# A hybrid encoder layer: norm weights, the left half of x tile 0 and three weight tiles per partition in one first transfer, issued by halves of the partitions on two queues

## The chip, the core and the metric

One Trainium2 chip, one of its cores. The metric is device time of one execution in microseconds (us), the median of several runs; the output must agree with the reference. The engines named below are TensorE (PE; its weight loads are shown apart, as PEld), VectorE (DVE), ScalarE (ACT), GpSimd (POOL) and SyncE (SP). Transfers are issued by SP, ACT or POOL and run on 16 DMA engines.

## The reference

One layer of a hybrid encoder on x of 512 positions by 1024 channels, in float32. The part that this change touches is the first norm and the start of the input projection:

```python
def rms_norm(x, g):
    xf = x.astype(jnp.float32)
    y = xf * lax.rsqrt(jnp.mean(xf * xf, axis=-1, keepdims=True) + EPS)
    return (y * g.astype(jnp.float32)).astype(x.dtype)
...
h = rms_norm(x, attn_norm_g[l])
proj = h @ w_in[l]          # 1024 x 2560
xr, gate, q, k, v = jnp.split(...)
```

Behind it come, in this order, a depthwise convolution and two gated linear recurrences (forward and backward) on xr, dilated attention with a relative bias on q, k and v, an output projection with residual, an MLP (1024 to 4096, squared ReLU, back to 1024) with residual, and a last norm.

## The kernel before

**Tiling.** Positions are on the free dimension (S = 512), channels on the partitions (P = 128), so x is eight channel tiles (KD = 8), each 128 x 512. The norm's gains are multiplied into x tile by tile; the division by the root mean square is done later, on the product.

**Three matmuls for one.** Each float32 operand is split into two parts of a narrower matmul format (FR): hi is the operand copied into that format, lo is the rest. A product is the sum hi x hi, hi x lo and lo x hi, three matmuls into the same accumulator in PSUM (`mm3`, lines 311 to 314). The order of every engine's work is written out by hand (a manual schedule for PE, ACT, DVE and POOL); each queue runs in program order.

**The start.** Lines 131 to 142 set constants, run one small Exp on ACT (`warm`, line 138, which brings a table load with it) and eight 128 x 128 warm-up matmuls of ones on PE (line 142; each shows as two passes). SP issues, in this order: line 335, x tile 0 and the eight gain columns (XG = 520 elements per partition) into the buffer `tw`; line 336, three 128-column weight tiles of channel tile 0 into the rest of the same buffer; line 339, the fourth weight tile (`w03`); line 341, x tile k with its three weight tiles, for k = 1 to 7. POOL copies the gains aside (`ag`, line 337).

**`cvx(k)`** (lines 347 to 368) makes the hi and lo parts of x tile k and of its weight tiles, on ACT and DVE. For k = 0: the hi part of x is made by halves, the left 256 columns on ACT (line 353) and the right 256 on DVE (line 354); the hi parts of weight tiles 0 and 1 on DVE (356), of tile 2 on ACT (357); then DVE subtracts for lo of x (363), lo of the three weight tiles (364) and, after ACT's copy of the fourth tile (366), its lo (367). `sq(k)` (372) squares x tile k on ACT for the mean square, `addsq` (375) adds the squares on DVE.

**The first projection** (lines 448 to 458) fills four PSUM accumulators `pxr[0..3]`, each 128 output channels by 512 positions. For k = 0 and 1 the order is: the three hi x hi matmuls of pxr[0..2], then the three hi x lo, then the three lo x hi (line 453); for k = 0 then the three of pxr[3] through `mm3`. For k of 2 and above, `mm3` for each of pxr[0..2].

The host lays the arrays out: `xw0` (line 1777) is the array that the transfers of lines 335 and 336 read.

Of the kernel before, what the change touches and what calls it, by code (L numbers as in the profile page):

```python
# [12 lines left out]
FT = mybir.dt.float32  # L13
FR = mybir.dt.float32r
AF = mybir.ActivationFunctionType
OP = mybir.AluOpType

P = 128
S = 512
D = 1024  # L20
KD = D // P
# [14 lines left out]
TH = S // 2  # L36
# [62 lines left out]
def hybrid_kernel(ctx: ExitStack, tc, xw0, xw, xn, w_in, w_v, w_out, w_up, w_dn, gates, vecs, bias, fg, out):  # L99
    nc = tc.nc  # L100
# [3 lines left out]
    work = ctx.enter_context(tc.tile_pool(name="work", bufs=1))  # L104
# [4 lines left out]
    act = nc.scalar.activation  # L109
    stt = nc.vector.scalar_tensor_tensor  # L110
    NG = 45

    def g_(name, dt=FT, shape=(P, S)):
        return work.tile(list(shape), dt, name=name, tag="g", bufs=NG)
# [4 lines left out]
    def ps_(name, tag):  # L119
        return psum.tile([P, S], FT, name=name, tag=tag, bufs={"pj": 4, "gs": 2, "et": 2}[tag])  # L120

    def f(t):
        return t.bitcast(FT)
# [7 lines left out]
    epsb = consts.tile([P, 1], FT, name="epsb")  # L131
# [3 lines left out]
    mhalf = consts.tile([P, 4], FT, name="mhalf")  # L135
    nc.gpsimd.memset(mhalf, -0.5)
    warm = consts.tile([P, 1], FT, name="warm")
    act(warm, epsb, AF.Exp)
    pwarm = ps_("pwarm", "et")
    one = nc.const_aps.tensor(1.0, [P, P], FT)  # L140
    for _ in range(8):
        nc.tensor.matmul(pwarm[:, :P], lhsT=one, rhs=one, start=True, stop=True)

    def softplus_consts():
# [166 lines left out]
    def mm3(o, a, b, first, last, on=False):  # L311
        nc.tensor.matmul(o, lhsT=a[0], rhs=b[0], start=bool(first), stop=False, skip_group_check=on)  # L312
        nc.tensor.matmul(o, lhsT=a[0], rhs=b[1], start=False, stop=False, skip_group_check=on)  # L313
        nc.tensor.matmul(o, lhsT=a[1], rhs=b[0], start=False, stop=bool(last), skip_group_check=on)  # L314
# [8 lines left out]
    h_hi = big.tile([P, KD, S], FR, name="h_hi", tag="bigA")  # L323
    h_lo = big.tile([P, KD, S], FR, name="h_lo", tag="bigB")

    XW, XG = S + 3 * P, S + KD
    ag = consts.tile([P, KD], FT, name="ag")
    xwt, w3 = [], []
    for k in range(KD):
        if 4 <= k < 7:  # L330
            xwt.append(stream.tile([P, 1024], FT, name="wraw", tag="wraw", bufs=3)[:, :XW])
        else:
            xwt.append(work.tile([P, 1024], FT, name="tw", tag="tw", bufs=4)[:, :XW if k else XG + 3 * P])
        if k == 0:
            nc.sync.dma_start(xwt[0][:, :XG], xw0[:, :XG])
            nc.sync.dma_start(xwt[0][:, XG:], xw0[:, XG:])
            nc.gpsimd.tensor_copy(ag, xwt[0][:, S:XG])
            w03 = g_("w03")[:, :P]
            nc.sync.dma_start(w03, w_in[3][:, :P])
        else:  # L340
            nc.sync.dma_start(xwt[k], xw[k - 1])
        if k == 6:
            nc.sync.dma_start(vt, vecs)

    sqx = {}

    def cvx(k):
        x, w = xwt[k][:, :S], xwt[k][:, S if k else XG:]
        g = ag[:, k:k + 1] if k else xwt[0][:, S:S + 1]
        hi, lo = g_("w3h", FR), g_("w3l", FR)  # L350
        if k < 2:
            c = (2 * P, 3 * P)[k]
            act(h_hi[:, k, :c], x[:, :c], AF.Copy, scale=g)
            nc.vector.tensor_scalar(h_hi[:, k, c:], x[:, c:], g, None, op0=OP.mult)
            if k == 0:
                nc.vector.tensor_copy(hi[:, :2 * P], w[:, :2 * P])
                act(hi[:, 2 * P:3 * P], w[:, 2 * P:], AF.Copy)
            else:
                nc.vector.tensor_copy(hi[:, :3 * P], w)
        else:  # L360
            act(h_hi[:, k, :], x, AF.Copy, scale=g)
            act(hi[:, :3 * P], w, AF.Copy)
        stt(h_lo[:, k, :], x, g, f(h_hi)[:, k, :], op0=OP.mult, op1=OP.subtract)
        nc.vector.tensor_tensor(lo[:, :3 * P], w, f(hi)[:, :3 * P], op=OP.subtract)
        if k == 0:
            act(hi[:, 3 * P:], w03, AF.Copy)
            nc.vector.tensor_tensor(lo[:, 3 * P:], w03, f(hi)[:, 3 * P:], op=OP.subtract)
        w3.append((hi, lo))

    def sq(k):  # L370
        sqx[k] = g_("sqx")
        act(sqx[k], xwt[k][:, :S], AF.Square)

    def addsq(k):
        nc.vector.tensor_tensor(sqx[0], sqx[0], sqx.pop(k), op=OP.add)

    cvx(0)
    sq(0)
    for k in range(1, KD):
        cvx(k)  # L380
        if 5 <= k < 7:
            next(spc)
        sq(k)
        if k >= 2:
            addsq(k - 1)
# [7 lines left out]
    def hk(k):  # L393
        return (h_hi[:, k, :], h_lo[:, k, :])

    def wk(c, k):
        if c < 3 or (c, k) == (3, 0):
            return tuple(t[:, c * P:(c + 1) * P] for t in w3[k])
        hi, lo = splits[c]
        return (hi[:, k * P:(k + 1) * P], lo[:, k * P:(k + 1) * P])  # L400
# [26 lines left out]
    def turned(ss, tag):  # L427
        pc = ps_("pcs", tag)
        for tt in range(4):
            nc.tensor.transpose(pc[:, tt * P:(tt + 1) * P], ss[:, tt * P:(tt + 1) * P], ident)  # L430
        return pc
# [16 lines left out]
    pxr = {t: ps_("pxr", "pj") for t in range(4)}  # L448
    for k in range(KD):
        if k < 2:  # L450
            for i, (a, b) in enumerate(((0, 0), (0, 1), (1, 0))):
                for t in range(3):
                    nc.tensor.matmul(pxr[t], lhsT=wk(t, k)[a], rhs=hk(k)[b], start=i == 0 and k == 0, stop=False)
            if k == 0:
                mm3(pxr[3], wk(3, 0), hk(0), True, False)
            continue
        for t in range(3):
            mm3(pxr[t], wk(t, k), hk(k), False, k == KD - 1)
            if k == KD - 1 and t == 0:
                sqt = turned(sqx[0], "et")  # L460

# [28 lines left out]
    xc, gt, gact = {}, {}, {}  # L490
# [252 lines left out]
    for n, (k, tt) in enumerate(steps):  # L743
        c = C_V + k // 2
        if k == 0:
            pv[tt] = ps_("pv", vtag[tt])
        hi, lo = splits[c]
# [511 lines left out]
    for w in OSEQ:  # L1259
        for i in range(4):  # L1260
            tt, k = i // 2, i % 2
# [260 lines left out]
    for half in range(2):  # L1522
# [5 lines left out]
        start = 0  # L1528
        if half == 0:
            start = 3  # L1530
# [161 lines left out]
        for j in range(7 * NQ):  # L1692
            _, w, q = seq[j]
# [32 lines left out]
        if half == 1:  # L1726
            b = 6 * NQ
# [89 lines left out]
```

## Time and profile before

| | us |
|---|---|
| median of 3 runs | 525.14 (524.99 to 525.32) |
| the profiled execution | 525.49 |
| its span, first to last instruction | 523.7 |
| PE busy | 517.1 (99%) |
| DVE busy | 430.4 (82%) |
| ACT busy | 352.2 (67%) |

The profile is of one execution. A row of its timeline reads: start, duration (both in us), engine, line of the kernel, operation, the tile written and those read, shapes, how many instructions were merged into the row, and in brackets the idle time just before with what ended it. SPq and ACTq are the instruction queues of SP and ACT, which show the issue of a transfer, not its data. Matmuls overlap, since they are pipelined, so that their starts tell the pace better than their durations. Before PE's first matmul and after its last one the span holds about 7.7 us in all.

### The profile page before, as it was taken

The numbers are of one execution on the slowest core, as the hardware profiler recorded it, in microseconds if no ns is written. First come the engines' busy times: TensorE is split into PE (matmuls) and PEld (weight loads), VectorE is DVE, ScalarE is ACT, GpSimd is POOL, SyncE is SP. The second block draws the span as 40 slices with busy tenths as digits, with TensorE's granted clock in tenths as the row PEclk, the third lists the DMA queues.
The fourth block names the chain that finished last, engine by engine and source line by source line (L and its number), as shares of the span: only waits on it lengthen the run. The fifth ranks groups of instructions, "written<-read, shape, count | busy, mean of one in ns | idle before, by whom it ended". The sixth has DMA issues, their size and how long they took to land.

```text
span 523.7 us, 8216 instructions
## 1 busy us (share of the span) xinstructions
PE 517.1 (99%) x3021; PEld 444.3 (85%) x3021; DVE 430.4 (82%) x668; ACT 352.2 (67%) x570; POOL 65.3 (12%) x89
## 2 busy tenths in 40 slices
PE   9999999999999999999999999999999999999995
PEld 8867888778777788899999888889999999888884
DVE  6899986788886898898789987789766978986885
ACT  7579946667857857586578666565667577655655
POOL 0173000000000321001300312001100300131000
PEclk9999999999999999999999999999999999999999
DMA  7636555266796499947595899976986497799704
GB/s 288 208 99 196 161 160 180 83 191 199 190 294 197 115 196 247 353 134 195 139 223 143 213 273 281 306 271 161 300 256 168 117 224 210 157 289 257 195 1 161
DMA packets 40329, 105.15 MB, mean 201 GB/s; under 512 B 5056, under 2 KB 13376, under 8 KB 40288
## 3 DMA queue, kind: packets, MB, share of 16 engines
q1 hardware_dynamic: 32448, 78.10, 44.5%
q0 software_dynamic: 7696, 26.32, 27.3%
q8 instruction: 24, 0.39, 0.3%
q10 hardware_dynamic: 144, 0.20, 0.1%
q14 instruction: 17, 0.14, 0.1%
HBM read 95.59 MB, written 4.29 MB: 191 GB/s over the span
## 4 chain that ended last, share of the span: by engine, by line
PE 99%; DVE 0%; issue 0%; DVEq 0%; ACT 0%; ACTq 0%
PE pu L314 10%; PE pu L312 10%; PE pu L313 10%; PE pd L314 10%; PE pd L312 10%; PE pd L313 10%; PE pqk L312 3%; PE pqk L314 3%; PE pqk L313 3%; PE pwo L312 3%; PE pwo L314 3%; PE pwo L313 3%; PE pav L942 2%; PE pt L842 2%; PE ps L806 2%; PE pp L312 1%
## 5 line engine op out<-in xcount | busy, mean ns | idle before, releaser
L269 DVE TENSOR_TENSOR wlo<-wraw,whi 128x1024 fp32r<-128x1024 f32 x71 | 86.6, 1220 | 24.0 <-ACT whi L247 23.9
L247 ACT ACTIVATE whi<-wraw 128x1024 fp32r<-128x1024 f32 x67 | 70.8, 1057 | 37.4 <-PE pd L314 18.4
L313 PE MATMUL pd<-wlo,ah 128*128 128x512 f32 (+1 forms) x195 | 75.2, 386 | 0.0
L312 PE MATMUL pd<-whi,ah 128*128 128x512 f32 (+1 forms) x195 | 75.2, 386 | 0.0
L314 PE MATMUL pd<-whi,al 128*128 128x512 f32 (+1 forms) x195 | 75.2, 386 | 0.0
L313 PE MATMUL pu<-hl,whi 128*128 128x256 f32 x224 | 63.4, 283 | 0.0
L314 PE MATMUL pu<-hh,wlo 128*128 128x256 f32 x224 | 63.4, 283 | 0.0
L312 PE MATMUL pu<-hh,whi 128*128 128x256 f32 x224 | 63.4, 283 | 0.0
L312 PE MATMUL pu<-h2h,whi 128*128 128x256 f32 (+1 forms) x200 | 60.1, 300 | 0.0
L313 PE MATMUL pu<-h2l,whi 128*128 128x256 f32 (+1 forms) x200 | 60.0, 300 | 0.0
L314 PE MATMUL pu<-h2h,wlo 128*128 128x256 f32 (+1 forms) x200 | 60.0, 300 | 0.0
L269 DVE TENSOR_TENSOR wlo<-tw,whi 128x1024 fp32r<-128x1024 f32 x37 | 45.2, 1221 | 17.7 <-ACT whi L247 17.7
L247 ACT ACTIVATE whi<-tw 128x1024 fp32r<-128x1024 f32 x38 | 40.1, 1058 | 24.9 <-PE pd L314 6.3
L312 PEld LDWEIGHTS pu<-hh,whi 128*128 128x128 f32 x224 | 43.0, 192 | 0.0
L313 PEld LDWEIGHTS pu<-hl,whi 128*128 128x128 f32 x224 | 43.0, 192 | 0.0
L314 PEld LDWEIGHTS pu<-hh,wlo 128*128 128x128 f32 x224 | 43.0, 192 | 0.0
L313 PEld LDWEIGHTS pd<-wlo,ah 128*128 128x128 f32 x195 | 36.6, 188 | 7.4
L312 PEld LDWEIGHTS pd<-whi,ah 128*128 128x128 f32 x195 | 36.6, 188 | 7.3
L314 PEld LDWEIGHTS pd<-whi,al 128*128 128x128 f32 x195 | 36.6, 188 | 7.4
L247 ACT ACTIVATE whi<-ts 128x1024 fp32r<-128x1024 f32 x24 | 25.4, 1060 | 25.2 <-PE pd L314 16.4
L313 PEld LDWEIGHTS pu<-h2l,whi 128*128 128x128 f32 x200 | 38.3, 191 | 1.3
L314 PEld LDWEIGHTS pu<-h2h,wlo 128*128 128x128 f32 x200 | 38.3, 191 | 1.3
(280 smaller groups left out, 1220.1 us busy)
## 6 DMA issues: line engine op xcount, KB each, us to landing
wraw<-in_w_up_dram SPq DMA_DIRECT2D x25, 512.0 KB, 4.8
ts<-in_w_dn_dram POOLq DMA_DIRECT2D x24, 512.0 KB, 13.5
wraw<-in_w_dn_dram SPq DMA_DIRECT2D x24, 512.0 KB, 8.7
tw<-in_w_up_dram SPq DMA_DIRECT2D x15, 512.0 KB, 6.7
tw<-in_w_up_dram POOLq DMA_DIRECT2D x15, 512.0 KB, 7.5
wraw<-in_w_in_dram SPq DMA_DIRECT2D x13, 512.0 KB, 4.3
ts<-in_w_dn_dram SPq DMA_DIRECT2D x8, 512.0 KB, 9.0
tw<-in_w_dn_dram SPq DMA_DIRECT2D x8, 512.0 KB, 7.0
```

Source lines behind the costliest of these rows:

```text
L247: act(hi, raws[i], AF.Copy)
L269: nc.vector.tensor_tensor(lo, r, f(splits[i][0]), op=OP.subtract)
L312: nc.tensor.matmul(o, lhsT=a[0], rhs=b[0], start=bool(first), stop=False, skip_group_check=on)
L313: nc.tensor.matmul(o, lhsT=a[0], rhs=b[1], start=False, stop=False, skip_group_check=on)
L314: nc.tensor.matmul(o, lhsT=a[1], rhs=b[0], start=False, stop=bool(last), skip_group_check=on)
L806: nc.tensor.matmul(psq[p, u][e][:, :NK], lhsT=qs_[p, a][r, P * qt:P * qt + P], rhs=kks[p][r, b, w:w + NK], start=i == 0, stop=i == 2)
L842: nc.tensor.transpose(pt[:, i * P:(i + 1) * P], en[h][qt][:, k:k + P], ident)
L942: nc.tensor.matmul(pav[p][a, co], lhsT=vs[:, jt, h * DH:(h + 1) * DH], rhs=et[h, jt][:, ci], start=jt == 0 and i == 0, stop=jt == 3 and i ...
```

## The change

- The host array `xw0` is laid out anew: the eight gain columns first, then the left half of x tile 0 (TH = 256 columns), the three weight tiles (384 columns), then the right half of x tile 0 and the fourth weight tile.
- The first transfer takes gains, left half and three weight tiles (XL = 648 elements, 2592 B per partition). Partitions 0 to 63 are issued by SP, partitions 64 to 127 by ACT. The small Exp that was first on ACT comes after ACT's issue.
- SP's second transfer brings the right half of x tile 0 and the fourth weight tile (384 elements per partition) into a buffer of its own, `x0r`. There is no third one: the x tiles 1 to 7 follow directly.
- For k = 0 the hi part of the left half of x is made on DVE and that of the right half on ACT; the hi part of weight tile 0 on ACT, of tiles 1 and 2 on DVE. The lo part of x and the squares are made in two halves.
- The three hi x hi matmuls of k = 0 become six of 256 columns: left halves of pxr[0..2], then right halves. The first of them alone clears the accumulator (`start`).
- Seven warm-up matmuls instead of eight.

```diff
-    act(warm, epsb, AF.Exp)
...
-    for _ in range(8):
+    for _ in range(7):
         nc.tensor.matmul(pwarm[:, :P], lhsT=one, rhs=one, start=True, stop=True)
...
-    XW, XG = S + 3 * P, S + KD
+    XW, XL = S + 3 * P, KD + TH + 3 * P
...
         if k == 0:
-            nc.sync.dma_start(xwt[0][:, :XG], xw0[:, :XG])
-            nc.sync.dma_start(xwt[0][:, XG:], xw0[:, XG:])
-            nc.gpsimd.tensor_copy(ag, xwt[0][:, S:XG])
-            w03 = g_("w03")[:, :P]
-            nc.sync.dma_start(w03, w_in[3][:, :P])
+            x0r = g_("x0r")
+            nc.sync.dma_start(xwt[0][:P // 2], xw0[:P // 2, :XL])
+            nc.scalar.dma_start(xwt[0][P // 2:], xw0[P // 2:, :XL])
+            act(warm, epsb, AF.Exp)
+            nc.sync.dma_start(x0r[:, :TH + P], xw0[:, XL:])
+            nc.gpsimd.tensor_copy(ag, xwt[0][:, :KD])
+            x0, w03 = (xwt[0][:, KD:KD + TH], x0r[:, :TH]), x0r[:, TH:TH + P]
...
+    lr = (slice(0, TH), slice(TH, S))
...
     def cvx(k):
...
+        if k == 0:
+            nc.vector.tensor_scalar(h_hi[:, k, lr[0]], x0[0], g, None, op0=OP.mult)
+            act(hi[:, :P], w[:, :P], AF.Copy)
+            nc.vector.tensor_copy(hi[:, P:3 * P], w[:, P:])
+            act(h_hi[:, k, lr[1]], x0[1], AF.Copy, scale=g)
+            for c, xc in zip(lr, x0):
+                stt(h_lo[:, k, c], xc, g, f(h_hi)[:, k, c], op0=OP.mult, op1=OP.subtract)
...
     def sq(k):
         sqx[k] = g_("sqx")
-        act(sqx[k], xwt[k][:, :S], AF.Square)
+        for c, xc in zip(lr, x0) if k == 0 else ((slice(0, S), xwt[k][:, :S]),):
+            act(sqx[k][:, c], xc, AF.Square)
...
             for i, (a, b) in enumerate(((0, 0), (0, 1), (1, 0))):
+                if i == k == 0:
+                    for c in lr:
+                        for t in range(3):
+                            nc.tensor.matmul(pxr[t][:, c], lhsT=wk(t, 0)[0], rhs=hk(0)[0][:, c], start=c is lr[0], stop=False, skip_group_check=True)
+                    continue
...
-    arrs["xw0"] = cont(np.concatenate([xT[0], cols(a["attn_norm_g"][0]), wx[0]], axis=1))
+    arrs["xw0"] = cont(np.concatenate([cols(a["attn_norm_g"][0]), xT[0][:, :TH], wx[0], xT[0][:, TH:], wi[:P, 3 * P:4 * P]], axis=1))
```

More of the change, by code (lines that the diff above doesn't have):

```diff
@@ L332, in hybrid_kernel @@
         else:
-            xwt.append(work.tile([P, 1024], FT, name="tw", tag="tw", bufs=4)[:, :XW if k else XG + 3 * P])
+            xwt.append(work.tile([P, 1024], FT, name="tw", tag="tw", bufs=4)[:, :XW if k else XL])
         if k == 0:
-            nc.sync.dma_start(xwt[0][:, :XG], xw0[:, :XG])
-            nc.sync.dma_start(xwt[0][:, XG:], xw0[:, XG:])
-            nc.gpsimd.tensor_copy(ag, xwt[0][:, S:XG])
-            w03 = g_("w03")[:, :P]
-            nc.sync.dma_start(w03, w_in[3][:, :P])
+            x0r = g_("x0r")
[5 more added lines that the diff above has]
+            x0, w03 = (xwt[0][:, KD:KD + TH], x0r[:, :TH]), x0r[:, TH:TH + P]
         else:
@@ L345, in hybrid_kernel @@
     sqx = {}
+    lr = (slice(0, TH), slice(TH, S))
     def cvx(k):
-        x, w = xwt[k][:, :S], xwt[k][:, S if k else XG:]
-        g = ag[:, k:k + 1] if k else xwt[0][:, S:S + 1]
+        x, w = (xwt[k][:, :S], xwt[k][:, S:]) if k else (None, xwt[0][:, KD + TH:])
+        g = ag[:, k:k + 1] if k else xwt[0][:, :1]
         hi, lo = g_("w3h", FR), g_("w3l", FR)
-        if k < 2:
-            c = (2 * P, 3 * P)[k]
+        if k == 0:
[5 more added lines that the diff above has]
+                stt(h_lo[:, k, c], xc, g, f(h_hi)[:, k, c], op0=OP.mult, op1=OP.subtract)
+        elif k == 1:
+            c = 3 * P
             act(h_hi[:, k, :c], x[:, :c], AF.Copy, scale=g)
             nc.vector.tensor_scalar(h_hi[:, k, c:], x[:, c:], g, None, op0=OP.mult)
[L355 to L359, printed above, removed]
+            nc.vector.tensor_copy(hi[:, :3 * P], w)
         else:
@@ L362, in cvx @@
             act(hi[:, :3 * P], w, AF.Copy)
-        stt(h_lo[:, k, :], x, g, f(h_hi)[:, k, :], op0=OP.mult, op1=OP.subtract)
+        if k:
+            stt(h_lo[:, k, :], x, g, f(h_hi)[:, k, :], op0=OP.mult, op1=OP.subtract)
         nc.vector.tensor_tensor(lo[:, :3 * P], w, f(hi)[:, :3 * P], op=OP.subtract)
@@ L451, in hybrid_kernel @@
             for i, (a, b) in enumerate(((0, 0), (0, 1), (1, 0))):
+                if i == k == 0:
[3 more added lines that the diff above has]
+                    continue
                 for t in range(3):
-                    nc.tensor.matmul(pxr[t], lhsT=wk(t, k)[a], rhs=hk(k)[b], start=i == 0 and k == 0, stop=False)
+                    nc.tensor.matmul(pxr[t], lhsT=wk(t, k)[a], rhs=hk(k)[b], start=False, stop=False, skip_group_check=True)
             if k == 0:
@@ L457, in hybrid_kernel @@
         for t in range(3):
-            mm3(pxr[t], wk(t, k), hk(k), False, k == KD - 1)
+            mm3(pxr[t], wk(t, k), hk(k), False, k == KD - 1, True)
             if k == KD - 1 and t == 0:
```

## The prediction

> **What bounds the kernel now.** I read the page first (span, busy shares, the chain that ended last), then the waits of PE, then the chain in order of time at its two ends.
>
> ```profile
> span 523.7 us, 8216 instructions
> PE 517.1 (99%) x3021; PEld 444.3 (85%) x3021; DVE 430.4 (82%) x668; ACT 352.2 (67%) x570; POOL 65.3 (12%) x89
> PE 99%; DVE 0%; issue 0%; DVEq 0%; ACT 0%; ACTq 0%
> PE pwarm L142 <- PEq L1806: 0.8, 1, 0.8
> 516.82 0.48 DVE x1n L1473
> 519.87 0.33 DVEq L1813
> ```
>
> The chain is PE from end to end. The only wait that PE shows is the 0.8 us before its first warm-up matmul; after the last matmul about 7 us of DVE, ACT and output are left. So the time is: when PE gets to its first useful matmul, plus a queue of matmuls without gaps, plus a tail. The change touches only the first of these, and a shift there should reach the end unreduced, since no later stage is seen to hold PE up. The rest is decided in the first 9 us, on PE (start, duration, engine, line, then what it writes and reads):
>
> ```profile
> 0.73 3.49 PEld L142 LDWEIGHTS pwarm<-const-float32-1.0 128*128 128x128 f32 x16 [0.73 <-issue]
> 4.41 0.93 PEld L453 LDWEIGHTS pxr<-h_hi,w3h 128*128 128x128 f32 x3 [0.18 <-ACT w3h L357]
> 4.44 1.62 PE L453 MATMUL pxr<-h_hi,w3h 128*128 128x512 f32 x3
> 5.00 1.05 PE L453 MATMUL pxr<-h_hi,w3h 128*128 128x512 f32 x2
> 5.85 1.34 PE L453 MATMUL pxr<-h_lo,w3h 128*128 128x512 f32 x3
> 6.28 0.91 PE L453 MATMUL pxr<-h_lo,w3h 128*128 128x512 f32 x2
> 7.03 0.84 PE L453 MATMUL pxr<-h_hi,w3l 128*128 128x512 f32 x3
> 8.39 0.84 PE L453 MATMUL pxr<-h_hi,w3h 128*128 128x512 f32 x3
> 9.07 0.84 PE L453 MATMUL pxr<-h_lo,w3h 128*128 128x512 f32 x3
> ...
> 6.00:7.00 1.00, 1.00 (x4) 0.79 (x3) 0.49 (x2) 0.62 (x2) 0.00 (x0) 1.00 1.01 380
> ```
>
> Durations overlap, so I go by starts. From 5.85 to 6.28 one matmul of 512 columns takes 0.43 us; from 8.39 to 9.07 three take 0.68, which is 0.227 each. So the array runs at about half speed until some 6.9 us (between 6.28 and 7.03 the pitch changes), although the window row for 6 to 7 us gives a granted clock of 1.00 (the value ahead of the DMA share 1.01): here the pitch is what counts. And from 4.41 on PE is dense: its weight loads wait 0.18 us for the ACT cast of line 357, never again. A microsecond of earlier start is therefore worth 0.227/0.427 = 0.53 us at the end as long as it falls into the slow stretch.
>
> What sets 4.41, from the timeline and the view of DMA issues (KB each, us to landing last):
>
> ```profile
> 0.73 0.39 SPq L335 DMA_DIRECT2D tw<-in_xw_dram  x1
> 1.18 0.41 SPq L336 DMA_DIRECT2D tw<-in_xw_dram  x1
> 1.64 0.42 SPq L339 DMA_DIRECT2D w<-in_w_in_dram  x1
> 2.11 1.38 SPq L341 DMA_DIRECT2D tw<-in_xw_dram  x3
> 3.50 0.36 DVE L354 TENSOR_SCALAR h_hi<-tw 128x256 fp32r<-128x256 f32 x1 [2.65 <-DMA tw<-in_xw_dram]
> 3.50 0.51 ACT L353 ACTIVATE h_hi<-tw 128x256 fp32r<-128x256 f32 x1 [1.27 <-DMA tw<-in_xw_dram]
> 4.00 0.31 ACT L357 ACTIVATE w3h<-tw 128x128 fp32r<-128x128 f32 x1
> 4.00 0.29 DVE L356 CAST w3h<-tw 128x256 fp32r<-128x256 f32 x1
> ...
> tw<-in_xw_dram SPq DMA_DIRECT2D x1, 260.0 KB, 2.7
> tw<-in_xw_dram SPq DMA_DIRECT2D x1, 192.0 KB, 2.8
> out_dram<-tw ACTq DMA_DIRECT2D x1, 192.0 KB, 2.4
> ```
>
> The 260 KB of x and gains land at 0.73 + 2.7 = 3.43 and work starts at 3.50; the 192 KB of weights land at 1.18 + 2.8 = 3.98 and the casts start at 4.00; the ACT cast ends at 4.31 and PE loads 0.10 later.
>
> **The change part by part.**
>
> **The transfers.** The first pair carries 128 rows of 2592 B, 324 KB; then come 192 KB (right half of x, fourth weight tile). Going from 260 KB to 452 KB moved the start of work by 0.50 us, so 0.0026 us per KB; 64 KB more than the old first transfer puts the pair at 3.50 + 0.17 = 3.67, and the next 192 KB at 4.00 + 0.17 = 4.17. The trace shows no transfer by halves and none from ACT's queue at the start; the nearest row is the ACT store of the end, 192 KB in 2.4 us. Bounds: not later than with everything behind it (4.17); not earlier than about 3.3, the 260 KB row's 3.50 less half of the 0.39 us issue. I take 3.67, the row of the same size class with the same 16 engines. A rule speaks against the halves: the Trainium skill, page "DMA: Bandwidth & Descriptors", section "Rules for kernel authors", says of two transfers to disjoint partition halves that they serialize on the same 16 engines, and to use one transfer. By that rule the halves bring only sequencer time and 3.67 stands; if they ran side by side the early bound 3.3 would. No run here shows it yet.
>
> **The issues.** SP issues one descriptor set fewer ahead of the x tiles: the pair's half, then the 192 KB, then x tile 1 at 1.64 where it was 2.11. ACT issues its half at 0.73 (0.39 by SP's rows), so the table load and the warm activation behind it slip:
>
> ```profile
> 0.73 1.28 ACT L138 ACT_TABLE_LOAD   x1 [0.73 <-PEq L1806]
> 2.02 0.20 ACT L138 ACTIVATE warm<-epsb 128x1 f32<-128x1 f32 x1
> 4.21 0.74 DVE L363 SCALAR_TENSOR_TENSOR h_lo<-tw,h_hi 128x512 fp32r<-128x512 f32 x1
> 4.87 0.55 DVE L364 TENSOR_TENSOR w3l<-tw,w3h 128x384 fp32r<-128x384 f32 x1
> 5.30 0.31 ACT L366 ACTIVATE w3h<-w 128x128 fp32r<-128x128 f32 x1 [0.99 <-DMA w<-in_w_in_dram]
> 5.51 0.61 ACT L372 ACTIVATE sqx<-tw 128x512 f32<-128x512 f32 x1
> 6.50 0.62 ACT L353 ACTIVATE h_hi<-tw,ag 128x384 fp32r<-128x384 f32 x1 [0.38 <-DMA tw<-in_xw_dram]
> 7.16 0.75 DVE L363 SCALAR_TENSOR_TENSOR h_lo<-tw,ag,h_hi 128x512 fp32r<-128x512 f32 x1
> 7.83 0.55 DVE L364 TENSOR_TENSOR w3l<-tw,w3h 128x384 fp32r<-128x384 f32 x1
> ```
>
> The load would end at 1.12 + 1.28 = 2.40 and the warm activation at 2.60, under the wait for data until 3.67: cost nothing. Without that cover it would be 0.39 us of ACT.
>
> **PE's start.** DVE scales the left half, 3.67 to 4.03 (0.36, L354's row); ACT casts 128 weight columns, 3.67 to 3.98 (0.31, L357's row); PE loads 0.10 later, at 4.13 where it was 4.41: **0.28 us earlier**. Weights 2 and 3 follow on DVE (0.29) to 4.32, at PE by 4.42, while PE wants them at 4.13 + 0.21 = 4.34, or at 4.47 if the opening gap of the old start (5.00 - 4.44 = 0.56 against 0.43, so 0.13) comes again: at most 0.08 us of wait. The right half: ACT from 4.17 for 0.51 to 4.68, at PE by 4.78; PE has done three left halves (0.64) by 4.77 to 4.90. No wait to speak of.
>
> **Six half matmuls for three.** The columns are the same; three more weight loads. Nothing shows 256 columns at the slow pitch; at full speed the counts of two windows of PE (busy, instructions, clock, DMA share, GB/s) bound the extra:
>
> ```profile
> 10.00:15.00 5.00, 5.00 (x24) 1.00 0.69 240
> 231.00:236.00 5.00, 5.00 (x44) 1.00 0.51 146
> ```
>
> 24 matmuls of 512 columns against 44 of 256 in 5 us: two halves take 9% more than a whole, 0.12 us on three at the slow pitch, 0.06 at the end. Nothing is the other bound, as warm-up loads keep a pitch of 3.49/16 = 0.218, which is the time of half a slow matmul; I take nothing.
>
> **What comes after.** h_lo in halves: about 0.45 each, to 4.77 and, behind the right half, 5.22; PE wants it at 4.13 + 0.13 + 1.28 = 5.54. The weight remainder (0.55) is done at 5.77, wanted at 6.8; the fourth tile (0.31 on ACT, 0.29 on DVE) at 6.1, wanted at 7.3. ACT's square in two pieces costs some 0.2 us more and hides in its 0.38 us wait for x tile 1. Tile 1 is ready at 7.12 (ACT), 7.91 and 8.38 (DVE); PE reached it at 8.39, 9.07 and 9.75 and will now be there 0.2 sooner: no new wait. One warm-up matmul less (two passes, 0.44): its loads end at 4.23 - 0.44 = 3.79, and the hole before the first real load is 0.34 us instead of 0.18.
>
> **The sum.** 0.28 us at the slow pitch is 0.28 x 0.53 = 0.15; without the opening gap of 0.13 another 0.07. I take 0.18. The profiled execution took 525.49 (1.8 around its span of 523.7), so 525.31; it was 0.35 slower than the median 525.14 of the three runs, which becomes 524.96, say **524.95**. The bounds on the landing move PE's start from 0.65 earlier (3.3) to 0.22 later (4.17): 0.35 gained to 0.12 lost.
>
> **The rivals.**
>
> **The pair lands only with what follows it (no change).** SP's second transfer lies right behind its half and shares the engines with ACT's half. In the worst case the pair is there at 4.17, PE starts at 4.63, 0.22 later: 525.14 + 0.12 = 525.25. For it: both queues use the same engines. Against: SP issues one transfer only at 1.18, 0.45 after the pair. That the change brings no earlier start at all is this case. 17%.
>
> **The half-speed stretch is renewed (slower).** The array turned fast some 6.1 us after its first warm-up matmul (0.77 to 6.9), having idled for no more than 0.18. If the longer hole (0.34, or 0.84 with the late pair) makes that count start anew at 4.13, full speed comes at 10.2, 3.3 us later, at 1 - 0.53 = 0.47 per us: 1.55 lost, 0.18 gained: 526.5. It decides at the first hole that is too long; the trace shows only that 0.18 is not. Against: 0.34 is still small beside the stretch. 8%.
>
> **ACT's half is late.** If the table load is put ahead of the transfer, ACT's half leaves 1.28 later, PE starts 1.0 later than before: 525.7, and with a hole of 1.6 us, 527.2. The load stands under line 138, that of the activation, so it should move with it. 3%.
>
> **Full speed comes early (faster).** If the array turned fast by 4.1, the twelve matmuls of tile 0 would end at 4.13 + 2.72 = 6.85 and tile 1 would start when ready, 7.2 instead of 8.39: 1.2 less, 523.95. Nothing in the change does this by itself, and three runs within 0.33 us speak against a moment that wanders. The Trainium skill, page "TensorE: Matmul & The Clock Gate", section "What's actually happening", calls the activity window free-running, so that the moment varies by run; by that rule this could happen, before and after alike. 4%.
>
> **How the numbers follow.** The forecast (0.1 to 0.35 us gained) has 68%. A measurement of this kernel can tell about 0.2%, 1.05 us: the forecast, the late pair and the milder late half are all within it, 86%; slower 10% (renewed stretch 8, worse late half 2); faster 4%. The range 524.5 to 525.5 takes the landing bounds, 524.8 to 525.25, and the scatter of runs (0.33 among three) at either end; it leaves out the early and renewed clock and the late half.
>
> **What would show it.** Right: DVE's and ACT's first data work near 3.67, both in one step; first load of line 453's successor near 4.13; pitch still 0.43 until about 6.9; tile 1 reached near 8.2 and the last matmul 0.2 earlier. Wrong: first work at 4.1 or later; a pitch of 0.43 beyond 7; ACT's table load ahead of its transfer; any wait of PE inside tile 0 or later.

## The result, and the profile after

| | before | after |
|---|---|---|
| median, us | 525.15 (14 runs, 524.61 to 525.79) | 527.38 (14 runs, 525.35 to 529.37) |
| ratio to before | | 1.0038, interval 1.0026 to 1.0050 |
| profiled execution, us | 525.49 | 527.60 |
| its span | 523.7 | 525.8 |
| start of its last matmul | 517.58 | 519.54 |

The kernel became slower by about 0.4%, and its executions scatter over 4 us where they scattered over 1.2. Four executions among those of this document ran at a granted clock of 0.64 to 0.75 and took 642 to 891 us; all medians and intervals here leave them out. The page of the kernel after:

```profile
span 525.8 us, 8221 instructions
PE 517.8 (98%) x3022; PEld 444.8 (85%) x3022; DVE 430.2 (82%) x669; ACT 352.4 (67%) x571; POOL 65.2 (12%) x89
```

Busy times are those of before; only the span is 2.1 us longer. Where the 2.1 us lie shows in the timeline of the first 11 us (columns as before):

```profile
0.73 0.55 ACTq L336 DMA_DIRECT2D tw<-in_xw_dram  x1
0.73 0.58 SPq L335 DMA_DIRECT2D tw<-in_xw_dram  x1
1.37 0.81 SPq L338 DMA_DIRECT2D x0r<-in_xw_dram  x1
4.44 0.37 DVE L354 TENSOR_SCALAR h_hi<-tw 128x256 fp32r<-128x256 f32 x1 [3.59 <-DMA tw<-in_xw_dram]
4.96 0.98 PE L462 MATMUL pxr<-h_hi,w3h 128*128 128x256 f32 x3 [0.87 <-DVE h_hi L354]
5.74 0.51 ACT L357 ACTIVATE h_hi<-x0r,tw 128x256 fp32r<-128x256 f32 x1 [1.01 <-DMA x0r<-in_xw_dram]
6.30 1.01 PE L462 MATMUL pxr<-h_hi,w3h 128*128 128x256 f32 x3 [0.36 <-ACT h_hi L357]
7.11 1.48 PE L465 MATMUL pxr<-h_lo,w3h 128*128 128x512 f32 x3
8.39 1.41 PE L465 MATMUL pxr<-h_hi,w3l 128*128 128x512 f32 x3
9.64 0.40 PE L311 MATMUL pxr<-h_hi,w3h 128*128 128x512 f32 x1
9.87 0.40 PE L312 MATMUL pxr<-h_lo,w3h 128*128 128x512 f32 x1
11.03 0.85 PE L465 MATMUL pxr<-h_lo,w3h 128*128 128x512 f32 x3
```

Each half takes 0.55 to 0.58 us to issue, where the whole first transfer of before (260 KB) took 0.39, and the transfer behind it 0.81. Work on the first pair begins at 4.44 instead of 3.50, work on the right half at 5.74. PE stands idle twice, 0.87 us ahead of the left halves and 0.36 ahead of the right ones. Then comes a second loss: from 7.11 to 8.39 three matmuls take 1.28 us, 0.43 each, so the array is still slow when it had long been fast before; at 9.64 to 9.87 a matmul takes 0.23. The row of 11.03 is the second group of x tile 1; it stood at 9.07. From there on the two traces run in parallel: 1.96 us apart at this group, 1.96 apart at the last matmul (before, then after):

```profile
517.58 0.28 PE L314 MATMUL pd<-whi,al 128*128 128x256 f32 x1
```

```profile
519.54 0.28 PE L313 MATMUL pd<-whi,al 128*128 128x256 f32 x1
```

From the start of that matmul to the end of the span it is 6.14 us before (ahead of the result it was put at about 7, which is too much) and 6.29 after; e9 takes up these 0.15.

How much is which loss: the trace's record of PE's clock turns to full at 6.89 us in the profile before and at 9.59 in the profile after. These 2.70 us at 0.47 per us, the prediction's price, are 1.27 of the 1.96. The remaining 0.69 is PE work that is simply late: the first matmul of the projection comes 0.52 later (4.96 for 4.44) and the second hole is 0.36, which at 0.53 per us make 0.47. The other 0.22 this sum does not place; a part is that the three right halves take 0.81 (6.30 to 7.11), where three of 0.213 make 0.64. The chain of the kernel after names the transfer that ends last (start, duration, what):

```profile
1.37 4.35 DMA x0r<-in_xw_dram
```

### The profile page after: what moved, and what is told of

Read it like the earlier page. It is cut to its first block, busy times and chain, and to the rows that moved or that the text cites. A ratio compares the mean times of both kernels' runs of the same rounds, so it can differ in the third digit from the quotient of the medians.

```text
span 525.8 us, 8221 instructions
## 1 busy us (share of the span) xinstructions
PE 517.8 (98%) x3022; PEld 444.8 (85%) x3022; DVE 430.2 (82%) x669; ACT 352.4 (67%) x571; POOL 65.2 (12%) x89
## 4 chain that ended last, share of the span: by engine, by line
PE 97%; DMA 1%; DVE 0%; ACT 0%; SPq 0%; issue 0%; DVEq 0%; ACTq 0%
PE pu L311 10%; PE pu L313 10%; PE pu L312 10%; PE pd L313 10%; PE pd L311 10%; PE pd L312 10%; PE pqk L311 3%; PE pqk L313 3%; PE pqk L312 3%; PE pwo L311 3%; PE pwo L313 3%; PE pwo L312 3%; PE pav L954 2%; PE pt L854 2%; PE ps L818 2%; PE pp L311 1%
```

## The experiments

All twelve, with their intervals; "first work" is DVE's scaling of x, which waits for both parts of the pair (in e4 ACT's cast of the weights, the first to need both; in the variants of the kernel before, DVE's work on the first transfer), "right half" the one that reads `x0r`, "full clock" the moment at which the clock record of the profiled execution turns to full, "profiled" its time. Medians are of 5 to 11 runs, the first row's of 14; the kernel before, run beside them on the same chips, had medians of 524.91 to 525.05. Each kernel has one profile, and its time can lie well off the median (e5: 525.38 and 526.89).

| kernel | median | ratio to before, 95% | first work | right half | full clock | profiled |
|---|---|---|---|---|---|---|
| after | 527.38 | 1.0038 (1.0026 to 1.0050) | 4.44 | 5.74 | 9.59 | 527.60 |
| e1 whole transfer | 525.32 | 1.0005 (0.9996 to 1.0014) | 3.74 | 4.22 | 6.73 | 525.54 |
| e4 by columns | 525.42 | 1.0007 (0.9998 to 1.0016) | 3.91 | 4.34 | 4.02 | 525.55 |
| e5 both halves on SP | 526.89 | 1.0032 (1.0023 to 1.0041) | 4.51 | 4.86 | 3.70 | 525.38 |
| e7 even and odd rows | 526.44 | 1.0032 (1.0020 to 1.0044) | 3.92 | 5.58 | 3.84, lost 7.25, back 10.66 | 527.74 |
| e2 PE kept busy | 526.08 | 1.0017 (1.0008 to 1.0026) | 4.68 | 5.65 | 6.33 | 526.08 |
| e8 before, halves alone | 526.88 | 1.0044 (1.0031 to 1.0057) | 4.08 | | 4.69 | 526.13 |
| e3 before, 4 warm-ups | 526.17 | 1.0026 (1.0015 to 1.0036) | 3.42 | | 7.42 | 525.72 |
| e6 before, 7 warm-ups | 524.91 | 1.0000 (0.9991 to 1.0008) | 3.44 | | 5.02 | 524.64 |
| e9 before, longer rows | 525.65 | 1.0009 (1.0001 to 1.0018) | 3.48 | | 6.52 | 525.78 |
| e10 e1 and early reads | 525.43 | 1.0008 (0.9998 to 1.0017) | 3.76 | 4.34 | 5.23 | 525.38 |
| e11 e1, one early read | 524.90 | 1.0002 (0.9993 to 1.0011) | 3.81 | 4.33 | 5.82 | 525.15 |
| e12 e11, two arrays | 524.98 | 0.9999 (0.9990 to 1.0008) | 3.79 | 4.34 | 4.45 | 524.74 |

The theory was: the halves land late, and the idle PE that follows puts off the full clock. The rivals: the new layout and order are late by themselves; the clock has no part in it.

**e1, the first transfer whole.**

```diff
-            nc.sync.dma_start(xwt[0][:P // 2], xw0[:P // 2, :XL])
-            nc.scalar.dma_start(xwt[0][P // 2:], xw0[P // 2:, :XL])
+            nc.sync.dma_start(xwt[0], xw0[:, :XL])
```

> The changed kernel with its first transfer issued whole, 128 partitions by SP alone; nothing else differs. Theory H (the two halves on two queues are what lands late): work on the first data begins near 3.7 us where the changed kernel begins at 4.42, PE's first load of the first projection near 4.1, and the time is 524.6 to 525.4, level with the kernel before. Rival L (the new layout and order of tile 0 are late by themselves, whoever issues them): first work stays at 4.2 or later and the time at 526.8 or more.

Its timeline:

```profile
0.73 0.39 SPq L335 DMA_DIRECT2D tw<-in_xw_dram  x1
1.17 0.42 SPq L337 DMA_DIRECT2D x0r<-in_xw_dram  x1
3.74 0.36 DVE L353 TENSOR_SCALAR h_hi<-tw 128x256 fp32r<-128x256 f32 x1 [2.88 <-DMA tw<-in_xw_dram]
4.22 0.51 ACT L356 ACTIVATE h_hi<-x0r,tw 128x256 fp32r<-128x256 f32 x1 [0.17 <-DMA x0r<-in_xw_dram]
4.25 1.62 PE L461 MATMUL pxr<-h_hi,w3h 128*128 128x256 f32 x6 [0.16 <-DVE h_hi L353]
```

Theory H holds. 3.74 and 4.22 are the prediction's 3.67 and 4.17; the six half matmuls run without a hole, and the whole loss is gone. So the sizes were right for a transfer of 128 partitions. But the earlier start (4.25 against 4.44, 0.16 at the last matmul) did not come out as time; e9 to e12 follow that up.

**e8, the halves alone in the kernel before.** The old first transfer (x tile 0 and gains, 260 KB) by halves, with the small Exp behind ACT's issue.

```diff
-            nc.sync.dma_start(xwt[0][:, :XG], xw0[:, :XG])
+            nc.sync.dma_start(xwt[0][:P // 2, :XG], xw0[:P // 2, :XG])
+            nc.scalar.dma_start(xwt[0][P // 2:, :XG], xw0[P // 2:, :XG])
+            act(warm, epsb, AF.Exp)
```

> The kernel before with one part of the change alone: its first transfer (x tile 0 and gains, 260 KB) is issued by halves of the partitions, by SP and ACT, with the small Exp behind ACT's issue; weights, order and eight warm-up matmuls as before. Theory H (the halves are the whole loss): first work at 4.1 to 4.3 us instead of 3.50, the weights behind it near 4.7, PE's first load near 5.1, and the median at 526 to 527.5 with a spread above 2 us. Rival L (the layout and the order of tile 0 take part in the loss): the median rises by less than 0.5 us.

First work 4.08, PE's first load 4.97, median 526.88: with e1 the same statement from the other side. The weights, the transfer behind the halves, were worked on at 4.56, where it was 4.00. In its profile the clock was full by 4.69, and yet it took 526.13. The chain shows another price of the halves: SP's issues get longer, so x tile 1 is issued at 3.14 instead of 2.11 and is the last transfer in the chain. And e8 has one transfer more than the kernel before, which goes with 0.44 us more after the last matmul (6.58 for 6.14; see the last section), so that not all of its 1.97 is the late landing.

```profile
0.73 0.60 SPq L334
1.32 0.06 issue
1.38 0.80 SPq L337
2.19 0.05 issue
2.24 0.86 SPq L340
3.10 0.04 issue
3.14 4.28 DMA tw<-in_xw_dram
```

**e4, split by columns; e5, both halves on one queue; e7, even and odd rows.** These ask what about the halves is slow: two queues, 64 rows, or neighbouring rows.

```diff
# e4
+            nc.sync.dma_start(xwt[0][:, :XL // 2], xw0[:, :XL // 2])
+            nc.scalar.dma_start(xwt[0][:, XL // 2:], xw0[:, XL // 2:XL])
# e5
+            nc.sync.dma_start(xwt[0][:P // 2], xw0[:P // 2, :XL])
+            nc.sync.dma_start(xwt[0][P // 2:], xw0[P // 2:, :XL])
# e7
+            nc.sync.dma_start(xwt[0][0:P:2], xw0[0:P:2, :XL])
+            nc.scalar.dma_start(xwt[0][1:P:2], xw0[1:P:2, :XL])
```

> The changed kernel with its first transfer split between SP and ACT by columns (324 elements of each row, all 128 partitions on both queues) instead of by partitions. Theory P (64 partitions at a time use only part of the ways into the memory, so that each half lands slowly): first work near 3.7 us and the time near 525. Rival Q (two transfers issued at the same time on two queues are prepared one after the other, whatever they hold): first work at 4.1 to 4.5 and the time 526.5 to 527.6, as in the changed kernel.

> The changed kernel with both halves of the partitions issued by SP, one after the other; ACT issues nothing. Theory P (64 neighbouring partitions at a time land slowly, on whatever queue): the pair is still late, first work at 4.2 us or later, time 526.5 to 527.8. Rival Q (what is late is two queues at once): first work at 3.7 to 3.9 and the time near 525.3, as with the whole transfer.

> The changed kernel with the two halves taken as even partitions (SP) and odd partitions (ACT) instead of the lower and the upper 64. Theory P (neighbouring partitions crowd one half of the ways into the memory): first work near 3.75 us, time 525.1 to 525.6. Rival R (a transfer of 64 rows is prepared and finished slowly, whichever rows they are): first work at 4.3 or later, time 526.5 to 527.8.

The issues of e4 (two queues, all rows), then of e5 (one queue, half the rows), from their timelines:

```profile
0.73 0.41 ACTq L336 DMA_DIRECT2D tw<-in_xw_dram  x1
0.73 0.39 SPq L335 DMA_DIRECT2D tw<-in_xw_dram  x1
```

```profile
0.73 0.59 SPq L335 DMA_DIRECT2D tw<-in_xw_dram  x1
1.37 0.58 SPq L336 DMA_DIRECT2D tw<-in_xw_dram  x1
```

Two queues at once cost no measurable time: e4 is as quick as e1, though its first work is 0.17 later (3.91 for 3.74). So the halving of the rows is the cause, not the second queue. e5 loses nearly what the change loses, and theory P's numbers came true in it, but its halves did not land slowly one by one. The views of DMA issues (last number: us from issue to landing, the median where there are two) show it; first e1, then e5:

```profile
tw<-in_xw_dram SPq DMA_DIRECT2D x1, 324.0 KB, 3.0
```

```profile
tw<-in_xw_dram SPq DMA_DIRECT2D x2, 162.0 KB, 3.0
```

In e5 the pair is late because a half of the bytes takes as long to land as the whole, and the second half leaves 0.64 later (1.37). On two queues both halves leave at 0.73, and it is the landing that differs; first the kernel after, then e7:

```profile
tw<-in_xw_dram ACTq DMA_DIRECT2D x1, 162.0 KB, 3.0
tw<-in_xw_dram SPq DMA_DIRECT2D x1, 162.0 KB, 3.6
```

```profile
tw<-in_xw_dram ACTq DMA_DIRECT2D x1, 162.0 KB, 2.7
tw<-in_xw_dram SPq DMA_DIRECT2D x1, 162.0 KB, 3.1
```

With even and odd rows the pair lands 0.5 us sooner: of the 0.7 us by which the change's pair is later than the whole transfer, about 0.2 goes with 64 rows of any kind (their issue takes 0.55 to 0.60), 0.5 with neighbouring rows on two queues. These are single profiles; e2, whose transfers are those of the change, had first work at 4.68 instead of 4.44. Theory P's first work in e7 came nearly true (3.92 for 3.75), its time did not: 526.44 lies beside rival R's range, for the next transfer, `x0r`, came late. Work on it began at 5.58. It was late in all three kernels of this layout with halves of the rows on two queues (after 5.74, e2 5.65, e7 5.58) and not on one queue (e5 4.86). In e8, also with halves on two queues, the transfer behind them landed 3.2 us after its issue, against 4.2 to 4.3 for `x0r`. Why the last rows of `x0r` hang there is not settled.

**e2, PE kept busy.** Nine warm-up matmuls and one more between left and right halves; the transfers are those of the change.

```diff
-    for _ in range(7):
+    for _ in range(9):
...
                     for c in lr:
+                        if c is lr[1]:
+                            nc.tensor.matmul(pwarm[:, :P], lhsT=one, rhs=one, start=True, stop=True)
```

> The changed kernel with nine warm-up matmuls instead of seven and one more of them between the left and the right halves of the first projection, so that PE is hardly idle while it waits; the transfers are untouched. Theory C (idle PE puts off the moment at which the array turns fast, and most of the 2.2 us lost is that): the array turns fast by 7.6 us after the start in any execution, and the time is 525.5 to 526.3 with a spread of about 1 us. Rival D (the data are late, and the clock has no part in it): the time stays within 0.3 of the changed kernel's 527.4 or rises by what the fillers delay.

Three useless matmuls make the kernel 1.3 us faster (527.38 to 526.08), although its data come as late (4.68, 5.65): theory C. Its two groups of half matmuls and the next group stand in the profile so:

```profile
5.20 0.98 PE L464 MATMUL pxr<-h_hi,w3h 128*128 128x256 f32 x3 [0.26 <-DVE h_hi L354]
6.26 0.63 PE L464 MATMUL pxr<-h_hi,w3h 128*128 128x256 f32 x3
6.74 0.97 PE L467 MATMUL pxr<-h_lo,w3h 128*128 128x512 f32 x3
```

From the profile after to this one the clock turns full 3.26 us earlier (6.33 for 9.59) and the last matmul starts 1.52 earlier (518.02 for 519.54): 0.47 per us, the price used above, though first work is also 0.24 later. What is left to the kernel before, 1.0 by the medians (525.05 beside it), is the lateness itself and, by e9, some 0.15 at the end.

**e3 and e6, fewer warm-ups in the kernel before** (4 and 7 instead of 8 in line 141's loop).

> The kernel before with four warm-up matmuls instead of eight, so that PE idles some 1.9 us ahead of its first load, which cannot move (it waits for data). Theory C: the idle stretch keeps a window of the clock from counting as busy in most executions; the median rises by 0.7 to 1.6 us, to 525.9 to 526.8, and the spread grows to 2 us or more. Rival D: no change, 525.0 to 525.3, since no work is later.

> The kernel before with seven warm-up matmuls instead of eight: PE idles 0.4 to 0.6 us ahead of its first load instead of 0.18. A window of the clock was seen to count with 0.41 us of idle time in it and not to count with 0.7. Theory C: that hole is still borne, median 525.0 to 525.4. Rival (any longer hole puts the clock off): 525.7 or more.

e3 moves no work and loses 1.1 us; e6 loses nothing. So the change's seventh warm-up was harmless, and a hole of 1.6 us is not. How much idle time PE may have shows in windows of 3.41 us that end where the clock turns. The view of windows gives length, PE's busy time (instructions), granted clock, DMA share and GB/s (the granted clock reads 1.00 ahead of the first clock record too, though the pitch of the matmuls there is that of half speed). First e5, then e3, each with a window after which the clock did or did not change:

```profile
0.29:3.70 3.41, 2.93 (x14) 1.00 0.43 118
3.70:7.11 3.41, 2.36 (x13) 1.00 0.97 300
```

```profile
0.60:4.01 3.41, 2.04 (x8) 1.00 0.58 164
4.01:7.42 3.41, 3.00 (x7) 1.00 0.96 344
```

And the kernel before:

```profile
0.06:3.47 3.41, 2.71 (x13) 1.00 0.49 140
3.47:6.89 3.42, 3.42 (x11) 1.00 0.91 310
```

After 2.93 (86%) and 3.00 (88%) the clock turned full, after 2.71 (79%) and 2.04 (60%) it stayed at half. Once full, it stayed so through a window of 2.36 (69%) in e5. In e7 it did not:

```profile
0.43:3.84 3.41, 3.08 (x14) 1.00 0.48 149
3.84:7.25 3.41, 1.91 (x11) 1.00 0.93 318
7.25:10.66 3.41, 3.41 (x10) 0.50 1.01 398
```

After a window with 1.91 us of work (56%) the clock fell back to half for the next 3.41 us, as the 0.50 of the last row says. Counted in the same way, with PE idle ahead of its first matmul, all fourteen profiles fit: the window that ended at the first turn to full had PE busy for 86% or more, the one before it for 79% or less. Whether the rise asks for a busy share or for no single hole above some 0.5 us is not told apart (the holes were at most 0.47 us in the one case and at least 0.70 in the other).

**e9, longer rows alone.** Why did e1 not gain? From its last matmul's start to the end of the span it took 6.34 us where before it was 6.14, which gives back the 0.16, and x tile 1 was worked on at 6.62 instead of 6.50 though it was issued 0.47 earlier. e9 gives the host array of the kernel before the change's row length, 4128 B; the last 128 elements are not read.

```diff
+    arrs["xw0"] = cont(np.concatenate([xT[0], cols(a["attn_norm_g"][0]), wx[0], wi[:P, 3 * P:4 * P]], axis=1))
...
+            nc.sync.dma_start(xwt[0][:, XG:], xw0[:, XG:XG + 3 * P])
```

> The kernel before with one thing of the change: the host array of x tile 0 has rows longer by 128 elements (4128 B instead of 3616 B), of which the transfers leave the last 128 unread; transfers, order and warm-up are as before. Theory A (the longer array, and the addresses of all arrays behind it, cost the 0.15 us at the very end and the later x tile 1 that the kernel with the whole first transfer showed): last matmul to end of span 6.25 us instead of 6.09, work on x tile 1 at 6.6 us instead of 6.5, median 525.2 to 525.5. Rival (they come from the new order of work): 6.1 us, 6.5 us, and the median within 0.15 of the kernel before.

Theory A holds for the end: 6.29 us (the expectation's 6.25 and 6.09 count to the start of the last instruction, 0.05 less). The time rose more than expected (525.65 for 525.2 to 525.5): a ratio of 1.0009 (0.5 us), whose interval begins at 1.0001 and so only just excludes no change. Work on tile 1 began at 7.60 in its one profile, an us later than expected, and PE's weight loads waited 0.31 us for it; so the 0.15 is not all that this run lost.

**e10, e11, e12, early reads.** ACT issues small transfers at the start that read 16 B of each row of x tiles 1 and 2 (e10) or 1 alone (e11) into a buffer that nobody uses; e12 is e11 with the second transfer's data in an array of their own. All three have e1's whole first transfer.

```diff
+            touch = consts.tile([P, KD, 4], FT, name="touch")
+            for j in range(2):                     # e11: j = 0 alone
+                nc.scalar.dma_start(touch[:, j, :], xw[j][:, :4])
...
-            nc.sync.dma_start(x0r[:, :TH + P], xw0[:, XL:])
+            nc.sync.dma_start(x0r[:, :TH + P], xr0)   # e12
```

> The changed kernel with the whole first transfer by SP, and two small transfers more, issued by ACT at the start, which read 16 B of each row of x tiles 1 and 2 into a buffer that nobody uses. Theory F (the first reads of an array are slow, which holds up x tile 1): work on x tile 1 begins at 6.2 us or earlier instead of 6.62, and the median falls by 0.1 to 0.4 us to 524.8 to 525.2. Rival (the small transfers only delay the first one): first work later than 3.74 by 0.1 us or more, tile 1 not earlier, median 525.3 to 525.8.

> The kernel with the whole first transfer by SP and one small transfer by ACT (16 B of each row of x tile 1 alone; the one with two such transfers had x tile 1 at 5.76 us but 6.69 us from the last matmul to the end, where SP waits for the transfers' semaphores one after the other and met that of the last store first). Theory W (the number of transfers sets the place of the last store's semaphore in that row): with one transfer less the tail is 6.2 to 6.3 us again, x tile 1 stays at 5.7 to 6.2, and the median is 524.8 to 525.2. Rival (the tail grows with ACT's early transfers themselves): tail 6.5 or more, median 525.3 or more.

> The same with the 384 elements of the second transfer (right half of x tile 0 and the fourth weight tile) in an array of their own, so that no row of the two arrays is 4128 B long. Theory A (it is the row length of 4128 B): the last matmul to the end takes 6.1 us, and the median falls by 0.15 against the one before it, to 524.6 to 525.0. Rival (it is the total size of the inputs, which moves the addresses behind): 6.25 us as before, median unchanged within 0.1.

Work on x tile 1 in e1, then in e11:

```profile
6.62 0.62 ACT L361 ACTIVATE h_hi<-tw,ag 128x384 fp32r<-128x384 f32 x1 [1.08 <-DMA tw<-in_xw_dram]
```

```profile
5.55 0.60 ACT L363 ACTIVATE h_hi<-tw,ag 128x384 fp32r<-128x384 f32 x1
```

Theory F holds as far as the arrival goes: x tile 1 is there an us sooner (5.76 in e10, 5.55 in e11, 5.57 in e12). e10 gives it back at the end, where 6.74 us pass after the last matmul's start; with one transfer less, e11 has 6.30, and e12 with no row of 4128 B has 6.13. Theories W and A hold for the end. Theory A's other half, a median lower by 0.15, did not show (524.98 for e11's 524.90), a difference that these runs hardly resolve. In time, e11 and e12 are level with the kernel before. No version beats it measurably.

## Why the prediction was wrong

- **The transfers: the step that failed.** It took 3.67 for the pair and 4.17 for what follows, and gave "not later than with everything behind it (4.17)" as a bound. Measured: 4.44 and 5.74. The estimate went by bytes, from rows of 128 partitions, and for a transfer of 128 partitions it was right (e1: 3.74 and 4.22). The late bound was none: it assumed that the way of issuing changes the order of bytes but not their rate or the time until they are reported as landed. The trace before had no transfer of 64 rows, and I took the nearest row instead of keeping the late end open. The Trainium skill's rule against halves (page "DMA: Bandwidth & Descriptors", section "Rules for kernel authors") pointed the right way; it says that halves bring nothing, and these runs show that they cost: the pair is worked on 0.7 us later than a whole transfer and 0.5 later than a split by columns on the same two queues.
- **The issues: wrong with it.** The prediction gave a half 0.39 us by rows of 128 partitions and put x tile 1's issue at 1.64. The halves took 0.55 and 0.58, the transfer behind them 0.81, and x tile 1 was issued at 2.23, later than before (2.11).
- **The rival of the renewed half-speed stretch** is what happened, with another count. It was reckoned for a hole of 0.34 us, or 0.84 with the late pair, after which a count of 6.1 us starts anew, and given 8%. The holes were 0.87 and 0.36 us, and no count of 6.1 starts anew at a hole (the full clock came 4.63 us after the end of the 0.87, and in e3 3.00 after one of 1.61): what fits the runs is windows of 3.41 us, of which one busy for 79% was too little and one of 86% enough. That its 10.2 for the full clock stands near the 9.59 measured is luck. Its price per us was right (0.47 between the kernel after and e2), its 526.5 too low since the arrival was late on top of it.
- **The moment of full clock wanders.** I took 6.9 us for fixed, and three runs within 0.33 us as speaking against a moment that wanders. In the kernel before and in e6, which moves no work, it lay at 6.89 and 5.02, each with its total: 525.49 and 524.64. 1.87 us apart, 0.85 us of time, 0.45 per us. In e7 the clock changed at 3.84, 7.25 and 10.66, 3.41 apart each time, and in every profile the last stretch of full clock lasts a whole number of such windows (515.41 us, 151 of them, in eleven; 518.83, 152, in two; 512.00, 150, in e7). The Trainium skill's rule (page "TensorE: Matmul & The Clock Gate", section "What's actually happening"), which I gave 4%, agrees: the windows are free-running and 3413 ns long. Windows of 3.41 us that may fall anywhere would account for both scatters, though no other execution's clock is on record: 1.2 us before (3.41 us at 0.45 are 1.5) and 4 us after, as windows that overlap the holes are lost. The rival's 523.95 was reached by no run: with the clock full at 4.45, e12 took 524.74.
- **"A shift there should reach the end unreduced": right.** 1.96 us at x tile 1, 1.96 at the last matmul.
- **0.53 us of time per us of earlier start in the slow stretch: the runs agree.** e1 starts PE 0.19 earlier (4.25 for 4.44), which makes 0.10, and its clock turns full 0.16 earlier (6.73 for 6.89), which at 0.47 makes 0.08; it is 0.16 ahead at the last matmul. The further 0.07 that the sum took for a missing opening gap did not come: e1's six half matmuls take 1.42 us (4.25 to 5.67), the three whole ones before took 1.41 (4.44 to 5.85).
- **ACT's table load behind its issue: right**, it ran from 1.31 and cost nothing. **One warm-up matmul less: right**, e6 shows no change.
- **No new wait for x tile 1: wrong where the clock is early.** In e4 the clock was full at 4.02; PE had done tile 0 and waited for tile 1, which came at 7.33; so this early clock still ended at 525.55. With x tile 1 touched early, e12 (full clock at 4.45) had 524.74.

## What to carry to other kernels

Do not take the price of a transfer of 64 partitions from rows of 128: here a half of the partitions took longer to issue than the whole (0.55 to 0.60 us for 0.39) and landed no sooner after it (3.0 us for 3.0), and with the other half on a second queue the pair was 0.7 us late. The split by columns cost no measurable time, and gained none. Ahead of the first matmul, count what a late operand costs twice: the wait, and the window of PE's clock that the wait spoils; useless matmuls in the hole bought the second part back here (e2). And where a trace has a slow stretch at the start, take its end as a draw, not as a constant, and compare kernels by many runs.

## What the runs showed of the hardware that was not expected

- A DMA of 64 partitions took 0.55 to 0.60 us to issue on SP or ACT in all five kernels that had one, one of 128 partitions 0.39 to 0.42 at the start, with 64 to 324 KB; the transfer issued by SP right behind two halves took 0.58 (one queue) or 0.80 to 0.81 (two).
- PE's clock fell back to half after a window in which PE was busy 56% of the time; it needed no idle window for that (e7, 3.84 to 7.25 us).
- Reading 16 B of each row of an array early made a later transfer from it usable about 1 us sooner (6.62 in e1; 5.76, 5.55 and 5.57 in e10 to e12). Why is not told.
- The span after the last matmul depends on the number of transfers in the whole program. At the end SP waits for their semaphores in a fixed order, some 0.06 us each, and the transfers take the semaphores in rotation. The last store has the last or last but one of the order in before, after, e1, e11 and e12; with one transfer more than before (e8) or two more than e1 (e10) it has the third, and seven waits are still to be made behind it: 7 x 0.06 = 0.42 us, the 0.4 that they lost there (e8 6.58 for 6.14, e10 6.74 for e1's 6.34).
- A host array with rows of 4128 B came with 0.15 us more at the end: 6.29 to 6.34 us from the last matmul's start in eight of the nine kernels that have it (e10, the ninth, is named above), 6.13 to 6.15 in before, e3, e6 and e12. SP's wait for the last store ends 2.67 us after its issue in after and e9, 2.50 and 2.51 in before and e12. The total size of the inputs is not it, since e12's is e1's; the row length and the places of the arrays in memory are not told apart.
